# A hybrid decoder step on one core: the sampled sequences' states loaded in both layouts, their update fused, and a second pair of buffers for two evacuation tiles

## The chip, the cores and the metric

The kernel runs on one core of a Trainium2 chip. The metric is the device time of one execution in microseconds (us); lower is better. A matrix product runs on TensorE (PE); VectorE (DVE), ScalarE (ACT) and GpSimd (POOL) work beside it. Loads are issued by SyncE (SP), stores mostly by ACT. Every engine takes its instructions in a fixed order, and a waiting instruction holds up everything behind it on that engine.

## The reference, cut to what matters

One layer is computed for a prompt of 1024 positions and, with the same weights, for 8 sampled sequences of 8 positions each (64 positions). Per layer: a normalised and modulated input, one wide product `h @ w_in`, a pooling branch, a Mamba-2 state-space branch (SSD), and two output products. The change touches only the state-space branch of the samples, where each sequence brings a recurrent state of 32 heads x 64 x 128:

```
acs = cumsum(dt * A)
y   = (C B^T * decay * dt) x   +  (C * exp(acs)) . h        # h: the state before
h   = h * exp(acs_last) + sum_j  B_j  w_in_j  x_j           # the new state, an output
```

`C . h` contracts over the state's 128 columns (n); the update scales the old state by one number per head and sequence and adds an outer product.

## The kernel before, in words

The work is done in stretches one after the other: the input and the first products (to about 120 us), the wide product `h @ w_in` (to about 798 us), the SSD of the prompt in 32 chunks with the output products of the branches woven in (to about 1075 us), and the last products.

The wide product is made in pairs of 128 columns. Each pair is one Strassen step (`strassen`, seven `product`s of 24 matmuls of 272 columns, lines L611 to L613 in before). The results leave PSUM by DVE (and ACT at L654) into four tiles of a pool with one buffer each: `s1`, `u2`, `u3` and `c2`. L622 is `add`, which writes `u2` from `s1` and `u3` from `u2`; L627 is `out`. The four tiles end as the pair's results: ACT applies the gate function to them (L723), and they are stored from there to DRAM (L725). So the next pair may write `u2` only when the store of the pair before has landed. A trace row drops the digits of a name: `u` is `u2` or `u3`, `h` is `h0`, and `whi`/`wlo` are the two halves into which ACT (L168) and POOL (L171) split each weight tile `raw` or `rawA`.

Beside the last ten pairs (`LAST = 10`, about 560 to 798 us) runs the work of the samples. First `dt_end` makes the decays; among others it makes `EbS`, the factor exp(acs_last) of every sequence and head, copied to all partitions (one product of ones, L1141, and one Exp, L1142). Then `ssd_samples` runs for four groups of 8 heads, one step at a time: `samples_beside` is called after each product of a pair and advances it. In a group:

- the decay matrix `dec` is loaded by SP (L1187), masked by two selects on POOL (L1195, L1196), passed through Exp on ACT (L1201), multiplied on DVE (L1249) and used by PE (`inner`, L1213);
- then for each half (4 sequences): the inputs are copied by POOL (L1261), turned by PE (L1264, L1266), and weighted by DVE into `xs` (L1268), `xh` (L1272, L1273) and `Bb` (L1276, L1278). `dec`, `xh` and `Bb` share a ring of three buffers with the tag `dec`;
- the four states of the half lie turned, 128 state columns on the partitions, 512 (head, channel) columns along them. PE multiplies them by `cz` (L1293), DVE scales them by `EbS` (L1298), and then for each sequence PE makes the outer product (L1288), DVE adds it (L1289) and ACT stores the new state (L1290). The states are loaded six tiles ahead (`h0`, `H0B = 6`, L1237), and turned back on the host.

The order on each engine in this stretch is set by a scheduler that simulates a timeline; it follows the code's order, priorities and buffer releases. PE's order and the rest are fixed in the built program.

Of the kernel before, what the change touches and what calls it, by code (L numbers as in the profile page):

```python
# [46 lines left out]
def tile_pool_ssd_step(  # L47
    ctx: ExitStack, tc: tile.TileContext,
    x_prompt, x_sample, state_pool, state_conv, state_ssm, c_prompt, c_sample,
    w_ada, b_ada, norm_g, w_in, conv_w, conv_b, dt_bias, a_log, d_skip, ssm_norm_g,  # L50
# [6 lines left out]
    def nm(s):  # L57
        uid[0] += 1
        return f"{s}_{uid[0]}"
# [38 lines left out]
    def PB():  # L98
        return psB.tile([P, 512], F32, tag="ps", name=nm("ps"))
# [435 lines left out]
    def pair_w(c0, c1, pri, early):  # L535
# [63 lines left out]
        return run  # L599
    prep_q = []  # L600

    turn = [0]
# [463 lines left out]

    H0B = 6


    def dt_end():  # L1070
# [14 lines left out]

        A = sp.tile([P, NH], F32, tag="A", name="A", bufs=1)
# [19 lines left out]
        yield  # L1106
        r, e, q, s2, p = tmp("xd", 2), tmp("xw", 1), tmp("h0", H0B), tmp("h0", H0B), tmp("hT", 1)
        V.tensor_scalar(r, x, 0.0, None, ALU.max)
# [110 lines left out]
    def spt(shape, tag, bufs, dt=F32):  # L1219
        return sp.tile(list(shape), dt, tag=tag, name=nm(tag), bufs=bufs)  # L1220

    def ssd_samples(g):
# [5 lines left out]
        load_E(E2, g)  # L1228
        dec = spt([P, 8, NS], "dec", 3)[:NS]
        decays(dec, g, NC)  # L1230
# [4 lines left out]
        def h0_load(j):  # L1235
            h0 = spt([P, 512], "h0", H0B)
            load(h0, state_ssm[g, j])  # L1237
            h0s[j] = h0
        h0_load(0)
        yield  # L1240
        px = PB()
# [7 lines left out]
        V.tensor_tensor(dec, dec, pc[:S, :S].unsqueeze(1).to_broadcast([S, 8, S]), ALU.mult)  # L1249
        for j in range(1, 4):  # L1250
            h0_load(j)
# [6 lines left out]
        for hf in range(2):  # L1258
# [4 lines left out]
            for q in range(4):  # L1263
# [20 lines left out]

            def update(b):
                h0 = h0s.pop(4 * hf + b)
                pu = PB()
                mm(pu, Bb[:96, b], xh[:96], start=True, stop=True)  # L1288
                V.tensor_tensor(h0, h0, pu, ALU.add)  # L1289
                store_(new_ssm_s[g, 4 * hf + b], h0)  # L1290
            po = PB()
            for b in range(4):
                mm(po[32 * b:32 * b + 32, :], cz[:, b, :], h0s[4 * hf + b], start=True, stop=True)  # L1293
            yo = spt([P, 512], "hT", 1)
            act(yo, po, AF.Copy)
            for b in range(4):
                hv = h0s[4 * hf + b].rearrange("p (h d) -> p h d", d=64)
                V.tensor_tensor(hv, hv, EbS[:, 4 * hf + b, 8 * g:8 * g + 8].unsqueeze(2).to_broadcast([P, 8, 64]), ALU.mult)  # L1298
                if b == 1:
                    yield  # L1300
            yield
            for b in range(4):
                update(b)
                if not hf:
                    h0_load(4 + b)
                if b < 3:
                    yield
# [240 lines left out]
    def to_ssd():  # L1548
        nonlocal right, sd, sp, mask, maskS, blkS, dtT, acT, wdT, wd3, blk3, Elb, EbS
# [10 lines left out]
        EbS = one([P, NB, NH], "EbS")  # L1560
# [6 lines left out]
    sd = sp = mask = maskS = blkS = dtT = acT = wdT = wd3 = blk3 = Elb = EbS = None  # L1567

# [13 lines left out]
    def samples_beside():  # L1582
        due[0] += 1
        if due[0] == 7 * LAST - 4:
            with behind(mybir.EngineType.SP):
                next(p_in)
# [383 lines left out]
    for i in range(8):  # L1970
# [34 lines left out]
        else:  # L2005
# [8 lines left out]

_INS = ['x_prompt', 'x_sample', 'state_pool', 'state_conv', 'state_ssm', 'c_prompt', 'c_sample', 'w_ada', 'b_ada',
        'norm_g', 'w_in', 'conv_w', 'conv_b', 'dt_bias', 'a_log', 'd_skip', 'ssm_norm_g', 'pool_w', 'pool_scale',
        'w_pool_out', 'w_ssm_out', 'w_o', 'final_g']
_OUTS = [((1, 1024, 1024), 'float32'), ((8, 8, 1024), 'float32'), ((512, 15), 'float32'),
         ((24, 128, 3), 'float32'), ((4, 128, 512), 'float32'), ((512, 8, 15), 'float32'),
         ((24, 128, 24), 'float32'), ((4, 8, 128, 512), 'float32')]  # L2020

# [5 lines left out]
def _lay(name, a):  # L2027
    if name == "state_ssm":
        return a.reshape(NB, NG, 512, P).transpose(1, 0, 3, 2)
    if name in ("state_conv", "state_pool"):  # L2030
        return a.reshape(-1, P).T
    return a


def _back(n, a):
    if n == 4:
        return a.transpose(0, 2, 1).reshape(1, 1, NH, 64, P)
    if n == 7:
        return a.transpose(1, 0, 3, 2).reshape(1, NB, NH, 64, P)
    if n == 2:  # L2040
        return a.T.reshape(1, 1, 15, DP)
    if n == 5:
        return a.transpose(1, 2, 0).reshape(1, NB, 15, DP)
    if n in (3, 6):
        return _conv_back(a, n)
    return a

# [19 lines left out]
```

## Time and profile before

| what | us |
|---|---|
| median of 3 runs (lowest to highest) | 1259.33 (1257.79 to 1262.46) |
| the profiled execution, its time | 1258.3 |
| its span in the profile | 1256.6 |
| PE busy | 1223.8 |
| DVE busy | 923.6 |
| ACT busy | 699.4 |
| POOL busy | 681.1 |

Read: PE is nearly always occupied, so the time is set by PE's work and by the places where PE waits or runs at a lower clock. The profiled execution lies 1.0 us under the median of the runs and within their spread.

### The profile page before, as it was taken

The page shows a single profiled execution, that of the slowest core. Times are in us where ns is not written, and L with a number is a line of the kernel's source. Part 1 is how long each engine was busy: PE and PEld are TensorE (multiplying, and loading weights), DVE is VectorE, ACT ScalarE, POOL GpSimd, SP SyncE. Part 2 cuts the span into 40 slices and gives each one's busy share as a digit, 9 for nine tenths or more (in the row PEclk, how much of TensorE's full clock was granted, in tenths as well). Part 3 has the DMA queues.
Part 4 walks back from the last instruction along what each step waited for, and adds up shares of the span by engine and source line. Part 5 has one row for each costly group of instructions (what it writes and reads, how often), then busy time and mean ns, then how long its engine had stood idle before and what let it go on. Part 6 is the DMA issues. An engine that isn't in the chain of part 4 may idle for free. (4 is left out here: it accounts for less than half of the span.)

```text
span 1256.6 us, 25313 instructions
## 1 busy us (share of the span) xinstructions
PE 1223.8 (97%) x9377; PEld 1151.2 (92%) x9377; DVE 923.6 (74%) x1521; ACT 699.4 (56%) x1616; POOL 681.1 (54%) x555
## 2 busy tenths in 40 slices
PE   7999999999999999999899999999999999999998
PEld 6779999999999999998789889999999999999786
DVE  4696689976989588974777776697767879666543
ACT  4675356575666656545444364787887768422211
POOL 1006668877888778664345444465565657455000
PEclk9999999999999999999899999999999999999999
DMA  9836555755555565444456545989666576485431
GB/s 358 264 120 221 138 164 148 199 197 152 159 184 194 162 168 161 152 137 134 147 162 210 168 140 172 330 295 319 207 193 200 181 225 200 144 289 170 151 109 51
DMA packets 208715, 234.85 MB, mean 187 GB/s; under 512 B 41242, under 2 KB 151174, under 8 KB 208591
## 3 DMA queue, kind: packets, MB, share of 16 engines
q1 hardware_dynamic: 154036, 159.51, 41.7%
q10 hardware_dynamic: 54554, 73.72, 17.0%
q8 instruction: 74, 1.21, 0.4%
q14 instruction: 51, 0.41, 0.1%
HBM read 158.56 MB, written 74.62 MB: 186 GB/s over the span
## 5 line engine op out<-in xcount | busy, mean ns | idle before, releaser
L171 POOL TENSOR_TENSOR wlo<-rawA,whi 128x512 fp32r<-128x512 f32 x120 | 190.5, 1593 | 157.4 <-ACT whi L168 79.8
L171 POOL TENSOR_TENSOR wlo<-raw,whi 128x512 fp32r<-128x512 f32 x92 | 150.6, 1644 | 125.2 <-ACT whi L168 115.3
L362 PE MATMUL mm<-Y,whi 128*128 128x352 f32 (+1 forms) x480 | 160.7, 335 | 0.6 <-DVE G L1876 0.2
L363 PE MATMUL mm<-Y,whi 128*128 128x352 f32 (+1 forms) x480 | 158.0, 329 | 0.4 <-DVE Y L1500 0.4
L364 PE MATMUL mm<-Y,wlo 128*128 128x352 f32 (+1 forms) x480 | 157.5, 328 | 0.0
L613 PE MATMUL mm<-Y,wlo 128*128 128x272 f32 x496 | 143.6, 290 | 1.9 <-POOL wlo L171 1.1
L611 PE MATMUL mm<-Y,whi 128*128 128x272 f32 x496 | 144.1, 291 | 0.7 <-ACT whi L168 0.7
L612 PE MATMUL ps<-Y,whi 128*128 128x272 f32 x496 | 143.1, 289 | 0.0
L611 PE MATMUL ps<-Y,whi 128*128 128x272 f32 x496 | 142.9, 288 | 0.0
L613 PE MATMUL ps<-Y,wlo 128*128 128x272 f32 x496 | 142.8, 288 | 0.0
L612 PE MATMUL mm<-Y,whi 128*128 128x272 f32 x496 | 142.4, 287 | 0.0
L1050 DVE SCALAR_TENSOR_TENSOR GA<-GA,cvT,GA 128x1112 f32<-128x1112 f32 x72 | 129.7, 1806 | 0.1
L168 ACT ACTIVATE whi<-rawA 128x512 fp32r<-128x512 f32 x125 | 77.9, 625 | 88.3 <-PE ps L612 44.1
L168 ACT ACTIVATE whi<-raw 128x512 fp32r<-128x512 f32 x96 | 58.9, 627 | 91.5 <-DVE raw L557 47.1
L611 PEld LDWEIGHTS mm<-Y,whi 128*128 128x128 f32 x496 | 93.6, 189 | 3.3 <-ACT whi L168 1.9
L613 PEld LDWEIGHTS mm<-Y,wlo 128*128 128x128 f32 x496 | 93.2, 188 | 2.9 <-POOL wlo L171 1.6
L611 PEld LDWEIGHTS ps<-Y,whi 128*128 128x128 f32 x496 | 93.4, 188 | 1.8 <-DVE c L627 0.8
L362 PEld LDWEIGHTS mm<-Y,whi 128*128 128x128 f32 x480 | 90.6, 189 | 4.1 <-DVE G L1876 2.3
L612 PEld LDWEIGHTS mm<-Y,whi 128*128 128x128 f32 x496 | 93.5, 188 | 0.7 <-issue 0.6
L612 PEld LDWEIGHTS ps<-Y,whi 128*128 128x128 f32 x496 | 93.3, 188 | 0.3
L613 PEld LDWEIGHTS ps<-Y,wlo 128*128 128x128 f32 x496 | 93.2, 188 | 0.0
L363 PEld LDWEIGHTS mm<-Y,whi 128*128 128x128 f32 x480 | 90.8, 189 | 2.7 <-DVE Y L1500 0.9
(440 smaller groups left out, 3760.7 us busy)
## 6 DMA issues: line engine op xcount, KB each, us to landing
rawA<-in_w_in SPq DMA_DIRECT2D x46, 512.0 KB
dec<-acs_d SPq DMA_DIRECT2D x32, 512.0 KB
xbc<-GA ACTq DMA_DIRECT2D x24, 512.0 KB
xb<-xbc SPq DMA_DIRECT2D x32, 384.0 KB
rawA<-in_w_in SPq DMA_DIRECT2D x32, 256.0 KB
pw<-in_w_ssm_out ACTq DMA_DIRECT2D x32, 256.0 KB
ws<-ph ACTq DMA_DIRECT2D x32, 256.0 KB
ws<-pw SPq DMA_DIRECT2D x32, 256.0 KB
```

The lines of the kernel that those rows point to most:

```text
L168: ins = act(hi[:, :, :ncols], raw[:, :, :ncols], AF.Copy)
L171: (eng or nc.gpsimd).tensor_tensor(lo[:, :, :ncols], raw[:, :, :ncols], hi[:, :, :ncols].bitcast(F32), ALU.subtract)
L362: mm(ps[:, :n], a, rh[k][:, o:o + n], start=(k == 0), stop=False)
L363: mm(ps[:, :n], a, rl[k][:, o:o + n], start=False, stop=False)
L364: mm(ps[:, :n], b, rh[k][:, o:o + n], start=False, stop=(k == nk - 1))
L611: mm(p, hi, ah, start=(k == 0), stop=False)
L612: mm(p, hi, al, start=False, stop=False)
L613: mm(p, lo, ah, start=False, stop=(k == 3))
L1050: V.scalar_tensor_tensor(d[:, :n], rp[:, k:k + n], cvT[:, 24 * k + mc:24 * k + mc + 1], d[:, :n], ALU.mult, ALU.add)
```

## The change

The state's tensor is handed to the program twice: `state_ssm` as it is (sequence, head, channel, state column) and `state_turned` in the layout of before. C's products (now L1302) read the turned one, from a new ring of four `hs` tiles, loaded four at a time. The update reads the plain one: a tile is now two heads of four sequences (128 partitions of head and channel, 4 x 128 columns), the outer product has its operands exchanged (L1293), and four SCALAR_TENSOR_TENSOR instructions (L1296) do `h0 * factor + product` in one pass, one for each sequence, with the factor taken as one number per partition from `E2`, a tile that is loaded anyway. The scaling by `EbS` and `EbS` itself go. The new state is written in the plain layout.

Room is made: `h0` has 5 buffers instead of 6, the `dec` ring 2 instead of 3, `yo` moves into the tag `xw`, `A` into `cz`, and the tile `p` of `dt_end` into `yt`. Of every two pairs beside the samples one takes `u2` and `u3` from a second place (`vu2`, `vu3`), except the last pair.

```diff
     def strassen(w, d0, d1, early=False):
         def tmp(tag):
+            if tag in ("u2", "u3") and beside[0] % 2 and beside[0] < LAST - 1:
+                return sp.tile([P, 2, SB], F32, tag="v" + tag, name=nm(tag), bufs=1)
             return pa.tile([P, 2, SB], F32, tag=tag, name=nm(tag))
...
-    H0B = 6
+    H0B = 5
...
-        own = tmp("xd", 2)[:NS, :256]
-        V.tensor_tensor(own.rearrange("p (b h) -> p b h", h=NH), a[:NS, 256:F].unsqueeze(1).to_broadcast([NS, NB, NH]),
-                        blk.unsqueeze(2).to_broadcast([NS, NB, NH]), ALU.mult)
-        pe = PB()
-        mm(pe[:, :256], ones[:NS], own, start=True, stop=True)
-        act(EbS.rearrange("p b h -> p (b h)"), pe[:, :256], AF.Exp, scale=-1.0)
...
-        dec = spt([P, 8, NS], "dec", 3)[:NS]
+        dec = spt([P, 8, NS], "dec", 2)[:NS]
...
         def h0_load(j):
-            h0 = spt([P, 512], "h0", H0B)
-            load(h0, state_ssm[g, j])
+            hf, q = divmod(j, 4)
+            h0 = spt([P, 4, P], "h0", H0B)
+            load(h0, state_ssm[0, 4 * hf:4 * hf + 4, 8 * g + 2 * q:8 * g + 2 * q + 2].rearrange("b h p n -> (h p) b n"))
             h0s[j] = h0
+        hts = {}
+
+        def turned_load(hf):
+            for b in range(4):
+                hts[b] = spt([P, 512], "hs", 4)
+                load(hts[b], state_turned[g, 4 * hf + b])
         h0_load(0)
+        turned_load(0)
...
-            xh = spt([P, 512], "dec", 3, F32R)
+            xh = spt([P, 512], "dec", 2, F32R)
...
-            Bb = spt([P, 4, P], "dec", 3, F32R)
+            Bb = spt([P, 4, P], "dec", 2, F32R)
...
-            def update(b):
-                h0 = h0s.pop(4 * hf + b)
+            def update(r):
+                h0 = h0s.pop(4 * hf + r)
                 pu = PB()
-                mm(pu, Bb[:96, b], xh[:96], start=True, stop=True)
-                V.tensor_tensor(h0, h0, pu, ALU.add)
-                store_(new_ssm_s[g, 4 * hf + b], h0)
+                mm(pu, xh[:96, r * P:(r + 1) * P], Bb[:96].rearrange("p b n -> p (b n)"), start=True, stop=True)
+                for b in range(4):
+                    cc_ = 32 * hf + 8 * b + 7
+                    V.scalar_tensor_tensor(h0[:, b, :], h0[:, b, :], E2[:, r, cc_:cc_ + 1],
+                                           pu[:, b * P:(b + 1) * P], ALU.mult, ALU.add)
+                store_(new_ssm_s[0, 4 * hf:4 * hf + 4, 8 * g + 2 * r:8 * g + 2 * r + 2]
+                       .rearrange("b h p n -> (h p) b n"), h0)
             po = PB()
             for b in range(4):
-                mm(po[32 * b:32 * b + 32, :], cz[:, b, :], h0s[4 * hf + b], start=True, stop=True)
-            yo = spt([P, 512], "hT", 1)
+                mm(po[32 * b:32 * b + 32, :], cz[:, b, :], hts[b], start=True, stop=True)
+            if not hf:
+                turned_load(1)
+            yo = spt([P, 512], "xw", 1)
             act(yo, po, AF.Copy)
-            for b in range(4):
-                hv = h0s[4 * hf + b].rearrange("p (h d) -> p h d", d=64)
-                V.tensor_tensor(hv, hv, EbS[:, 4 * hf + b, 8 * g:8 * g + 8].unsqueeze(2).to_broadcast([P, 8, 64]), ALU.mult)
-                if b == 1:
-                    yield
             yield
```

The scheduler sets the whole stretch anew. Outside about 540 to 800 us the order on all engines is as before. Three places matter for the prediction. First DVE in the second half of group 0, before. `xw` is `xs`, `dec` at L1273 and L1278 are `xh` and `Bb`, `u2`, `s1` and `c2` are tiles of a pair:

```order
L1268 TENSOR_TENSOR xw_1276_8230<-ps_1274_8223,wd3_7194 96x512
L1276 TENSOR_TENSOR bt_1278_8235<-ps_1275_8228,bt_1278_8235 32x128
L1273 TENSOR_TENSOR dec_1277_8232<-xw_1276_8230,dec_1277_8232 32x512
L1278 TENSOR_TENSOR dec_1279_8238<-bt_1278_8235,blk3_7195 96x512
L1298 TENSOR_TENSOR h0_1252_8113<-h0_1252_8113,EbS_7197 128x512
L1298 TENSOR_TENSOR h0_1254_8119<-h0_1254_8119,EbS_7197 128x512
L1298 TENSOR_TENSOR h0_1266_8174<-h0_1266_8174,EbS_7197 128x512
L1298 TENSOR_TENSOR h0_1270_8211<-h0_1270_8211,EbS_7197 128x512
L622 TENSOR_TENSOR u2_1286_8252<-s1_1285_8251,ps_1294_8306 128x272
L1289 TENSOR_TENSOR h0_1252_8113<-h0_1252_8113,ps_1295_8322 128x512
```

and the same place on DVE now (L1273, L1278, L1281 and L1283 are before's L1268, L1273, L1276 and L1278, and L625 is L622):

```order
L1273 TENSOR_TENSOR xw_1281_8246<-ps_1279_8239,wd3_7194 96x512
L1281 TENSOR_TENSOR bt_1283_8251<-ps_1280_8244,bt_1283_8251 32x128
L1283 TENSOR_TENSOR dec_1284_8254<-bt_1283_8251,blk3_7195 96x512
L1278 TENSOR_TENSOR dec_1282_8248<-xw_1281_8246,dec_1282_8248 32x512
L1296 SCALAR_TENSOR_TENSOR h0_1259_8129<-h0_1259_8129,hst_1214_7886,ps_1298_8306 128x128 x4
L625 TENSOR_TENSOR u2_1293_8275<-s1_1292_8274,ps_1301_8329 128x272
L1296 SCALAR_TENSOR_TENSOR h0_1261_8138<-h0_1261_8138,hst_1214_7886,ps_1302_8343 128x128 x4
L1296 SCALAR_TENSOR_TENSOR h0_1273_8196<-h0_1273_8196,hst_1214_7886,ps_1303_8350 128x128 x4
```

The four passes with `EbS` are gone from between `Bb` and the next pair's `u2`, and the updates follow at once.

Second, SP's queue at the start of group 1, with the waits of each load, before (`dec_8505` is group 1's decay matrix, `h` a state, `hst` the group's inputs):

```order
L1237 DMA h_1270_8211<-in_state_ssm 128x512 [waits DMAHW4_49,DMAHW0_49,DVE_49]
L1237 DMA h_1326_8521<-in_state_ssm 128x512 [waits DMAHW3_49,DVE_49]
L543 DMA rawA_8577<-in_w_in 128x4x256 [waits Pool_49]
L1237 DMA h_1330_8533<-in_state_ssm 128x512 [waits DMAHW5_49,DMAHW1_49,DVE_49]
L1225 DMA hst_8500<-xbc_175 128x6x64 [waits DMAHW2_49,PE_49,Pool_49]
L1187 DMA dec_8505<-acs_d 64x8x64 [waits PE_49]
L1237 DMA h_1331_8535<-in_state_ssm 128x512 [waits DMAHW6_49,DMAHW4_49,DVE_49]
```

and now, with the four turned loads ahead of it:

```order
L1235 DMA h_1332_8547<-in_state_ssm 128x4x128 [waits DMAHW4_49,DVE_49]
L1222 DMA hst_8526<-xbc_175 128x6x64 [waits Pool_49]
L1242 DMA hs_8549<-in_state_turned 128x512 [waits DMAHW2_49,PE_49]
L1242 DMA hs_8551<-in_state_turned 128x512 [waits DMAHW3_49,PE_49]
L1242 DMA hs_8553<-in_state_turned 128x512 [waits PE_49]
L1242 DMA hs_8555<-in_state_turned 128x512 [waits DMAHW5_49,PE_49]
L1184 DMA dec_8531<-acs_d 64x8x64 [waits DMAHW0_49,PE_49]
L1235 DMA h_1340_8567<-in_state_ssm 128x4x128 [waits DMAHW6_49,DMAHW2_49,DVE_49]
```

Both wait for PE, but not for the same matmul: with three buffers `dec` took the place of the first half's `Bb`; with two it takes that of the second half's `xh`, which PE reads until the last update of the group before.

Third, POOL at the group-0 decay, before:

```order
L171 TENSOR_TENSOR wlo_7784<-raw_7677,whi_7783 128x512
L1195 AFFINE_SELECT dec_7895<-dec_7895 64x512
L171 TENSOR_TENSOR wlo_7788<-rawA_7545,whi_7787 128x512
L1196 AFFINE_SELECT dec_7895<-dec_7895 64x512
L171 TENSOR_TENSOR wlo_7855<-rawA_7850,whi_7854 128x512
```

and now:

```order
L171 TENSOR_TENSOR wlo_7778<-raw_7676,whi_7777 128x512
L1192 AFFINE_SELECT dec_7889<-dec_7889 64x512
L1193 AFFINE_SELECT dec_7889<-dec_7889 64x512
L171 TENSOR_TENSOR wlo_7782<-rawA_7544,whi_7781 128x512
L171 TENSOR_TENSOR wlo_7849<-rawA_7844,whi_7848 128x512
```

The two selects now stand together, and one weight split has moved behind them.

More of the change, by code (lines that the diff above doesn't have):

```diff
@@ L600, in tile_pool_ssd_step @@
     prep_q = []
+    beside = [0]
     turn = [0]
@@ L1249, in ssd_samples @@
         V.tensor_tensor(dec, dec, pc[:S, :S].unsqueeze(1).to_broadcast([S, 8, S]), ALU.mult)
-        for j in range(1, 4):
+        for j in range(1, 3):
             h0_load(j)
@@ L1283, in ssd_samples @@
             yield
[L1285 to L1286 removed]
+            def update(r):
+                h0 = h0s.pop(4 * hf + r)
                 pu = PB()
[L1288 to L1290 removed]
+                mm(pu, xh[:96, r * P:(r + 1) * P], Bb[:96].rearrange("p b n -> p (b n)"), start=True, stop=True)
[5 more added lines that the diff above has]
+                       .rearrange("b h p n -> (h p) b n"), h0)
             po = PB()
             for b in range(4):
[L1293 to L1294 removed]
+                mm(po[32 * b:32 * b + 32, :], cz[:, b, :], hts[b], start=True, stop=True)
+            if not hf:
+                turned_load(1)
+            yo = spt([P, 512], "xw", 1)
             act(yo, po, AF.Copy)
[L1296 to L1306 removed]
+            yield
+            for q in range(4):
+                j = 4 * hf + q
+                update(q)
+                if j + 3 < 8:
+                    h0_load(j + 3)
+                if q < 3:
                     yield
@@ L1548, in to_ssd @@
     def to_ssd():
-        nonlocal right, sd, sp, mask, maskS, blkS, dtT, acT, wdT, wd3, blk3, Elb, EbS
+        nonlocal right, sd, sp, mask, maskS, blkS, dtT, acT, wdT, wd3, blk3, Elb
         right.__exit__(None, None, None)
@@ L1559, in to_ssd @@
         wd3, blk3, Elb = one([96, 2, NH], "wd3"), one([96, 4], "blk3"), one([P, NC, NH], "Elb")
-        EbS = one([P, NB, NH], "EbS")
         right = tc.tile_pool(name="sp", bufs=2, side="right", reuse_waits="tile")
@@ L1566, in tile_pool_ssd_step @@
     right_all = []
-    sd = sp = mask = maskS = blkS = dtT = acT = wdT = wd3 = blk3 = Elb = EbS = None
+    sd = sp = mask = maskS = blkS = dtT = acT = wdT = wd3 = blk3 = Elb = None
     first()
@@ L1583, in samples_beside @@
         due[0] += 1
+        beside[0] = int(due[0]) // 7
         if due[0] == 7 * LAST - 4:
@@ L2045, in _back @@
         return _conv_back(a, n)
+    if n == 4:
+        return a.transpose(0, 2, 1).reshape(1, 1, NH, 64, P)
     return a
@@ L2056 @@
     for name in _INS:
-        a = _np.ascontiguousarray(_lay(name, _np.asarray(inputs[name])))
+        a = _np.ascontiguousarray(_lay(name, _np.asarray(inputs["state_ssm" if name == "state_turned" else name])))
         arrays[f"in_{name}"] = a
```

18 lines of the change are left out of this document (7 added, 11 removed).

## The prediction, made before the changed kernel ran

> **What bounds the kernel now.** I read the page first, then the busy times by stretches of 40 us, then PE's waits in the stretch that the change touches. The page says that PE is occupied:
>
> ```profile
> PE 1223.8 (97%) x9377; PEld 1151.2 (92%) x9377; DVE 923.6 (74%) x1521; ACT 699.4 (56%) x1616; POOL 681.1 (54%) x555
> ```
>
> The columns below are the stretch and its length, busy time (and instructions) of PE, weight loads, DVE, ACT and POOL, granted clock, share of the DMA engines, GB/s.
>
> ```profile
> 520.00:560.00 40.00, 40.00 (x322) 39.99 (x321) 32.09 (x54) 21.04 (x44) 28.05 (x28) 1.00 0.48 157
> 560.00:600.00 40.00, 36.61 (x285) 33.97 (x283) 21.83 (x48) 22.11 (x46) 16.00 (x13) 0.98 0.44 131
> 600.00:640.00 40.00, 35.64 (x244) 30.98 (x240) 33.36 (x55) 17.57 (x38) 16.62 (x13) 0.90 0.45 141
> 720.00:760.00 40.00, 36.32 (x289) 33.90 (x288) 29.53 (x55) 22.72 (x48) 19.24 (x16) 1.00 0.43 148
> 840.00:880.00 40.00, 40.00 (x332) 37.81 (x331) 30.90 (x51) 29.32 (x78) 22.49 (x26) 1.00 0.94 314
> ```
>
> Before and after the samples' stretch PE is full; in it PE is idle some 10% of several rows, and at 600 to 640 the clock is below 1.00. Nothing there is full: DVE has 22 to 33 of 40 us. So PE waits for latency, for chains of small instructions in a fixed order, and what can be won is what it waits. PE's waits from 560 to 800 us, and the three stretches with a lower clock:
>
> ```profile
> PE ps L1213 <- DVE dec L1249: 3.1, 2, 2.3
> PE ps L1288 <- DVE u L622: 2.8, 1, 2.8
> PE ps L1288 <- DVE dec L1273: 2.7, 2, 1.3
> PE mm L613 <- POOL wlo L171: 1.8, 4, 0.7
> PE ps L1245 <- ACT s L654: 1.4, 1, 1.4
> PE mm L611 <- ACT whi L168: 0.8, 1, 0.8
> PE ps L1288 <- DVE h L1289: 0.2, 1, 0.2
> ...
> 590.00:600.00 10.00, 6.61 (x58) 5.95 (x56) 4.10 (x10) 8.85 (x21) 4.68 (x4) 0.90 0.65 184
> 600.00:610.00 10.00, 9.58 (x60) 7.10 (x57) 7.72 (x15) 3.37 (x8) 1.49 (x1) 0.76 0.08 29
> 630.00:640.00 10.00, 7.74 (x48) 7.43 (x48) 9.61 (x20) 6.32 (x15) 3.56 (x4) 0.83 0.52 156
> ```
>
> The waits add up to 12.8 us. The clock costs at most 10 x (0.10 + 0.24 + 0.17) = 5.1 us more. Some 18 us are thus all that this change can win; PE's own work hardly changes.
>
> The clock fell after the two longest waits, the first and second row here, and not after the others:
>
> ```profile
> 599.13 0.59 PE L1213 MATMUL ps<-dec,xd 64*64 64x64 f32 x6 [2.35 <-DVE dec L1249]
> 632.26 0.79 PE L1288 MATMUL ps<-dec,dec 96*128 96x512 f32 x1 [2.81 <-DVE u L622]
> 741.08 0.68 PE L1213 MATMUL ps<-dec,xd 64*64 64x64 f32 x16 [0.74 <-DVE dec L1249]
> ```
>
> The Trainium skill (TensorE: Matmul & The Clock Gate, "What's actually happening") has the clock halved after an idle window of about 3.4 us. By that rule waits of 2.35 and 2.81 us would leave it alone, and the 3.4 us of clock in my sum would stay lost; the trace shows it falling after them, so the measurement decides.
>
> **Why DVE is late there.** These are DVE's groups of 560 to 800 us (count, busy us, mean ns, idle before), then single instructions:
>
> ```profile
> L1298 DVE TENSOR_TENSOR h<-h,EbS 128x512 f32<-128x512 f32 x32 | 29.6, 982 | 0.4 <-PE ps L1293 0.3
> L1289 DVE TENSOR_TENSOR h<-h,ps 128x512 f32<-128x512 f32 x32 | 21.1, 676 | 1.9 <-PE ps L1288 1.9
> L622 DVE TENSOR_TENSOR u<-s,mm 128x272 f32<-128x272 f32 x9 | 3.9, 436 | 21.7 <-DMA gp<-u 10.3 <-DMA z<-u 5.4 <-DMA gs<-u 5.3
> ...
> 619.93 0.44 DVE L622 TENSOR_TENSOR u<-s,mm 128x272 f32<-128x272 f32 x1 [3.74 <-DMA z<-u]
> 623.85 6.73 DVE L1298 TENSOR_TENSOR h<-h,EbS 128x512 f32<-128x512 f32 x4
> 738.36 0.44 DVE L622 TENSOR_TENSOR u<-s,mm 128x272 f32<-128x272 f32 x1 [8.23 <-DMA gp<-u]
> ```
>
> Two things: DVE stands 21 us for `u2`, whose last store has not landed, and the scaling passes take 29.6 us. Before 632.26 both come together: 3.74 us for `u2`, then 6.73 for four passes.
>
> **The change part by part.** The rows that price DVE's work (ns least, median, most):
>
> ```profile
> L1298 DVE TENSOR_TENSOR h<-h,EbS x32: 676/682/3811, 603.4 to 767.9; 128x512 f32<-128x512 f32 x32
> L1289 DVE TENSOR_TENSOR h<-h,ps x32: 623/675/690, 609.7 to 776.4; 128x512 f32<-128x512 f32 x32
> L1312 DVE TENSOR_TENSOR yt<-ps,hst x8: 275/279/285, 615.1 to 777.0; 128x128 f32<-128x128 f32 x8
> L1316 DVE TENSOR_TENSOR xd<-xd,yt x8: 277/294/810, 615.4 to 777.6; 128x128 f32<-128x128 f32 x8
> ```
>
> Out go 29.6 + 21.1 = 50.7 us. In come 128 SCALAR_TENSOR_TENSOR of 128x128 with one operand in PSUM. The trace has none with a PSUM operand; the nearest row is L1312, same size, one operand in PSUM: 128 x 0.279 = 35.7 us. As the other end I take L1298's stretching, mean over least: 128 x 0.277 x 982 / 676 = 51.5. I take 35.7: rows with a PSUM operand (L1289, L1312) spread by 11% at most, those with both in SBUF stretch up to 5.6-fold (L1298) and 2.9-fold (L1316). So DVE gains 15 us, the longest pieces above all, or nothing.
>
> The Trainium skill (SBUF — State Buffer, "Who interferes with whom") says that a DVE instruction with two SBUF inputs contends with a GpSimd instruction that reads SBUF; the trace agrees, 3811 ns at most in L1298 against 690 in L1289. It does not say whether a per-partition factor in SBUF counts as the second input; if it did, the upper end would hold and DVE would gain nothing.
>
> *The wait for group 0's decay, 2.35 us, and the clock behind it.* By the order 93 product matmuls stand between L1245 and L1213 now, 76 before: 17 x 40 / 322 = 2.1 us of cover. The lost `EbS` steps shorten the chain too. Gain 2.35. But on POOL both selects now come ahead of a weight split that PE waited for already:
>
> ```profile
> 589.74 0.62 SPq L1187 DMA_DIRECT2D dec<-acs_d  x1
> 592.87 1.09 POOL L1195 TENSOR_SCALAR_AFFINE_SELECT dec<-dec 64x512 f32<-64x512 f32 x1 [0.17 <-DMA dec<-acs_d]
> 595.16 1.10 POOL L1196 TENSOR_SCALAR_AFFINE_SELECT dec<-dec 64x512 f32<-64x512 f32 x1
> ```
>
> That split is 1.1 us later: loss 1.1. Of the clock (3.4 here) I take half, 1.7. Net +2.95.
>
> *632.26.* Both causes go (a second `u2`, no passes): 2.81 + 1.7 of clock = +4.5.
>
> *The two waits for `xh` (2.7).* L1273 no longer stands behind the passes: +2.7. But the first update now follows C's products after 12 product matmuls (1.5 us) in both halves of group 0, where 36 and 14 stood; I take 0.5 us lost in each. Net +1.7.
>
> *736 to 741 us.* The 0.74 stood behind the 8.23 us for `u2`; the 1.4 is a PSUM bank that waits for ACT, which now has one table change fewer there: +2.1.
>
> *The weight waits, 1.8 + 0.8:* half of what is left beside the one above, +0.8. *The `EbS` product on PE:* one product less, which runs as two matmuls of 256 columns; at 40 / 322 = 0.124 us for one of 272 columns that is +0.25.
>
> *The ring of two.* Group 1 to 3's decay load now waits for PE's last update of the group before. From there: load 592.87 - 0.17 - 589.74 = 3.0; two selects 2.2 and one instruction between them 1.2; table 1.28 and Exps 2.0 (below); product 0.7, as L1289; sum 10.4 us. PE has 106 to 113 product matmuls in between by the order, 13.2 us or more. So PE needn't wait; ACT and POOL may, in order, with weight splits behind them. I take 0.8 us for each group, -2.5.
>
> ```profile
> 679.06 1.28 ACT L1201 ACT_TABLE_LOAD   x1 [0.45 <-ACT u L723]
> 680.36 0.35 ACT L1201 ACTIVATE dec<-dec,acT 64x64 f32<-64x64 f32 x1
> 682.05 0.34 ACT L1201 ACTIVATE dec<-dec,acT 64x64 f32<-64x64 f32 x1
> ```
>
> *Transfers.* 32 turned loads of 256 KB are 8.4 MB more; at 600 to 640 us a share of 0.45 moved 141 GB/s, so they add 27 us of all engines over 200, 0.13 to a share of some 0.5. The states now move in pieces of 512 bytes, which costs the issuing engine 0.2 us more each (L1386, such pieces, against L1290):
>
> ```profile
> L1386 SPq DMA_DIRECT2D sz<-z x32: 518/530/1559, 799.5 to 1071.2; - x32
> L1290 ACTq DMA_DIRECT2D out<-h x32: 338/344/891, 610.4 to 777.1; - x32
> ...
> SPq L543 <- POOL wlo L171: 188.2, 34, 17.7
> SPq L1237 <- DMA out<-h: 107.7, 22, 18.5
> ```
>
> On ACT that is 6.4 us of 240 in which it works about half: hidden by its idle time. On SP the 32 turned loads stand ahead of weight loads, which already wait for free buffers (first row), so they are early; the state loads wait for stores to land (second row), now with five buffers. If that cover went, DVE's updates would wait, and PE behind them. I count 0.
>
> Sum: 2.95 + 4.5 + 1.7 + 2.1 + 0.8 + 0.25 - 2.5 = 9.8 us. From the profiled execution, 1258.3, that gives 1248.5; the median of the runs lies 1.0 higher, so for a median I say 1249.5. About 0.5%, 6.3 us, is what a measurement of this kernel can tell from no change.
>
> **The rivals.**
>
> *DVE is not relieved* (51.5 us of updates). For: the factor is read from SBUF, and POOL works in the stretch. Against: L1289's narrow spread. Left are the start, half of 632, 0.74 and the -2.5: 2.95 + 2.25 + 0.74 - 2.5 = 3.4, so 1256. Chance 0.15.
>
> *The new order brings its own waits:* all eight halves wait about 1.3 us for `xh`, as 2.7 / 2 shows, because the updates stand so close behind. For: 12 product matmuls are 1.5 us and the chain has five instructions on three engines. Against: the last six halves have 12 to 31 between and DVE is emptier. 9.8 + 1.0 - 8 x 1.3 = 0.4, so 1259. Chance 0.13.
>
> *The ring of two makes it slower.* If the chain of 10.4 us takes 16, PE waits 2.8 at three group starts and loses 1.7 of clock each, 13.5 in all, and the gain of 12.3 without this term is gone; from there on it is slower, and at 18 by 3 x 6.5 - 12.3 = 7.2 us, 1266.5. For: POOL and ACT take it in order, behind weight splits and gate functions, and the turned loads are in the queue just ahead. Against: 3 us of slack and 0.13 more of DMA. Chance 0.12, of which 0.08 is slower by over 0.5%.
>
> **How the numbers follow.** My forecast has the remaining 0.60, with a range of its own from 1242 to 1253. Everything won would be 1259.3 - 12.8 - 5.1 - 0.25 = 1241, the low end; the high end takes in the first two rivals and leaves out the third: 1259. Faster by over 0.5% (under 1253): 0.60 and a third of the first rival, 0.65; slower: 0.08 and 0.02 of the second rival, 0.10; the rest, 0.25, within.
>
> **What would show it.** Right: no L1298; the new updates at about 280 ns with little spread; the idle time before the first `u2` of a pair gone except in the last pair; no wait of 2 us or more at L1213 or at the update matmul, and clock 1.00 from 600 to 640; the samples' stretch some 10 us shorter, the others as long as before. Wrong: waits of PE at L1213 of groups 1 to 3 behind the decay's load; update matmuls that wait for `xh`; updates stretched while POOL works; or POOL and ACT standing at the decay with weight splits late behind them.

## The result, and the profile after

The changed kernel takes 1245.1 us in the median (1241.7 to 1249.0, 4 runs) against 1259.9 for the kernel before on the same chip: a ratio of 0.9883, 95% interval 0.9846 to 0.9919. Two later comparisons gave 0.9906 [0.9888, 0.9924] and 0.9914 [0.9894, 0.9933]. So it is faster by about 1%, 11 to 15 us; the forecast was 1249.5. The profiled execution took 1249.0 us, the longest of the first four.

PE stays the bound, with 2.9 us less of occupied time:

```profile
PE 1220.9 (98%) x9375; PEld 1148.8 (92%) x9375; DVE 912.6 (73%) x1584; ACT 694.1 (56%) x1611; POOL 678.2 (54%) x555
```

The same stretches as before (columns: stretch and length, busy time of PE, weight loads, DVE, ACT, POOL, granted clock, DMA share, GB/s):

```profile
560.00:600.00 40.00, 38.09 (x296) 34.72 (x294) 22.58 (x52) 20.23 (x45) 17.06 (x14) 0.96 0.45 125
600.00:640.00 40.00, 39.62 (x315) 35.63 (x308) 30.82 (x78) 22.85 (x50) 22.22 (x18) 1.00 0.84 256
640.00:680.00 40.00, 39.32 (x306) 37.45 (x305) 29.66 (x72) 12.70 (x26) 16.12 (x15) 1.00 0.80 246
680.00:720.00 40.00, 37.83 (x277) 34.03 (x277) 26.86 (x66) 19.30 (x44) 15.30 (x13) 0.91 0.64 195
720.00:760.00 40.00, 40.00 (x325) 37.24 (x324) 27.41 (x69) 20.67 (x46) 21.57 (x18) 1.00 0.60 181
...
590.00:600.00 10.00, 8.09 (x65) 6.23 (x63) 3.93 (x9) 6.14 (x17) 4.66 (x4) 0.84 0.60 157
600.00:610.00 10.00, 10.00 (x79) 9.15 (x72) 9.07 (x23) 3.92 (x8) 3.61 (x3) 0.98 0.65 208
```

From 600 to 640 PE has 39.62 us of work at full clock, where it had 35.64 at 0.90; 720 to 760 is full. Two stretches have a lower clock than before: 560 to 600, with 0.96 (0.98 before), and 680 to 720, with 0.91 (1.00 before). PE's waits from 560 to 800 us:

```profile
PE ps L1210 <- DVE dec L1254: 2.1, 1, 2.1
PE mm L614 <- POOL wlo L171: 1.8, 2, 1.7
PE ps L1293 <- DVE dec L1278: 0.9, 2, 0.7
PE mm L363 <- DVE Y L1507: 0.4, 1, 0.4
```

They add up to 5.2 us, against 12.8. (L1210 is the inner product, L1293 the update matmul, L614 a product with the low part of a weight; L1213, L1288 and L613 before.) DVE's new updates, and the first `u2` of a pair (ns least, median, most; then one update's four; then busy us, mean ns, idle before):

```profile
L1296 DVE SCALAR_TENSOR_TENSOR h<-h,hst,ps x128: 334/342/349, 604.8 to 766.0; 128x128 f32<-128x128 f32 x128
...
604.82 1.11 DVE L1296 SCALAR_TENSOR_TENSOR h<-h,hst,ps 128x128 f32<-128x128 f32 x4
...
L1296 DVE SCALAR_TENSOR_TENSOR h<-h,hst,ps 128x128 f32<-128x128 f32 x128 | 35.1, 340 | 5.2 <-PE ps L1293 5.2
L625 DVE TENSOR_TENSOR u<-s,mm 128x272 f32<-128x272 f32 x9 | 3.9, 431 | 5.9 <-ACT whi L168 5.7
```

The updates have hardly any spread, and no store stands before `u2` any more.

The wait of 2.1 us is that of group 2's decay. Its chain, from the load's issue to PE (start, us, engine, line, operation, idle time before):

```profile
669.17 1.97 SPq L1184 DMA_DIRECT2D dec<-acs_d  x1
...
675.71 1.09 POOL L1192 TENSOR_SCALAR_AFFINE_SELECT dec<-dec 64x512 f32<-64x512 f32 x1 [4.72 <-DMA dec<-acs_d]
...
679.25 1.09 POOL L1193 TENSOR_SCALAR_AFFINE_SELECT dec<-dec 64x512 f32<-64x512 f32 x1
...
682.93 2.02 ACT L1198 ACTIVATE dec<-dec,acT 64x64 f32<-64x64 f32 x8
...
685.77 1.12 PE L1210 MATMUL ps<-dec,xd 64*64 64x64 f32 x16 [2.12 <-DVE dec L1254]
```

The load is issued at 669.17 and the first select can start at 675.71; two weight splits stand between the selects. From issue to PE it is 16.6 us. Behind this wait the clock falls, to 0.78 from 680 to 690 and 0.88 from 690 to 700: 10 x (0.22 + 0.12) = 3.4 us. In the second and third profile of the changed kernel the wait is 1.4 and 1.2 us, and the clock stays at 1.00 from 680 to 720.

All kernels of the study, with all their runs (those of the kernel before are of the three later comparisons). The last two columns split the mean time: what the mean granted clock leaves out of 1250 us, and the rest.

| kernel | runs | median us | ratio to before, 95% | clock lost, us | rest, us |
|---|---|---|---|---|---|
| before | 51 | 1257.7 | 1 | 8.4 | 1249.1 |
| after | 14 | 1245.5 | 0.9883, 0.9906, 0.9914 | 3.7 | 1242.0 |
| before, second `u2`, `u3` only | 12 | 1258.9 | 1.0004 [0.9991, 1.0017] | 6.9 | 1251.7 |
| before, no passes | 6 | 1248.2 | 0.9932 [0.9916, 0.9948] | 5.6 | 1243.1 |
| before, ring of two | 11 | 1255.2 | 0.9980 [0.9972, 0.9989] | 7.2 | 1247.6 |
| layout, ring of three | 11 | 1255.2 | 0.9976 [0.9961, 0.9992] | 6.3 | 1248.2 |
| layout, ring of three, decay held | 6 | 1251.4 | 0.9949 [0.9929, 0.9969] | 6.9 | 1243.5 |
| layout, ring of two | 12 | 1248.9 | 0.9930 [0.9908, 0.9952], 0.9939 [0.9919, 0.9958] | 4.7 | 1244.4 |
| after, ring of three, four states | 6 | 1250.7 | 0.9942 [0.9930, 0.9955] | 5.0 | 1245.5 |
| after, inner product later | 6 | 1247.0 | 0.9922 [0.9904, 0.9941] | 3.8 | 1244.2 |
| after, one split on DVE | 6 | 1247.1 | 0.9920 [0.9903, 0.9938] | 4.4 | 1242.4 |

Of the 11.7 us between the means of before and after (1257.4 and 1245.7) some 7 are waits and work and 4.7 are clock. That the clock came back because the waits went is shown only in part. By stretches of 20 us, the profile of the kernel before loses 5.2 us of clock from 560 to 800, and the three of the changed kernel lose 5.2, 1.8 and 0. The profile before loses another 1.7 us at 1090 to 1110 (0.99 and 0.84), where the order is the same in both kernels and no wait of PE is listed; the three of the changed kernel lose nothing there.

### The profile page after: what moved, and what is told of

Read it like the earlier page. It is cut to its first block, busy times and chain, and to the rows that moved or that the text cites. A ratio compares the mean times of both kernels' runs of the same rounds, so it can differ in the third digit from the quotient of the medians.

```text
span 1247.3 us, 25450 instructions
## 1 busy us (share of the span) xinstructions
PE 1220.9 (98%) x9375; PEld 1148.8 (92%) x9375; DVE 912.6 (73%) x1584; ACT 694.1 (56%) x1611; POOL 678.2 (54%) x555
## 5 line engine op out<-in xcount | busy, mean ns | idle before, releaser
L614 PE MATMUL mm<-Y,wlo 128*128 128x272 f32 x496 | 143.7, 290 | 2.8 <-POOL wlo L171 2.0
L613 PE MATMUL ps<-Y,whi 128*128 128x272 f32 x496 | 143.7, 290 | 0.0
L614 PE MATMUL ps<-Y,wlo 128*128 128x272 f32 x496 | 143.3, 289 | 0.0
L613 PE MATMUL mm<-Y,whi 128*128 128x272 f32 x496 | 142.5, 287 | 0.0
L614 PEld LDWEIGHTS mm<-Y,wlo 128*128 128x128 f32 x496 | 93.3, 188 | 4.6 <-POOL wlo L171 2.5
L613 PEld LDWEIGHTS mm<-Y,whi 128*128 128x128 f32 x496 | 93.5, 188 | 0.8 <-issue 0.6
L613 PEld LDWEIGHTS ps<-Y,whi 128*128 128x128 f32 x496 | 93.8, 189 | 0.2
L614 PEld LDWEIGHTS ps<-Y,wlo 128*128 128x128 f32 x496 | 93.8, 189 | 0.0
```

The source lines that it names most:

```text
L613: mm(p, hi, al, start=False, stop=False)
L614: mm(p, lo, ah, start=False, stop=(k == 3))
```

## Experiments

**The second buffers alone.** The kernel before, with this in `strassen` (and the counter `beside` of the pairs):

```diff
+            if tag in ("u2", "u3") and beside[0] % 2 and beside[0] < LAST - 1:
+                return sp.tile([P, 2, SB], F32, tag="v" + tag, name=nm(tag), bufs=1)
             return pa.tile([P, 2, SB], F32, tag=tag, name=nm(tag))
```

> The kernel before, with the second buffers for u2 and u3 alone; layout, scaling passes and ring of three stay. Account of the prediction (each of the two causes would do at 632, the passes alone make the other waits): DVE no longer stands 3.7 us at 619.9, so the wait of 2.8 us at the update of 632 and half or all of its clock (1.7 to 3.4 us) go, and of the waits at 736 and 741 some 2 us: 5 to 8 us faster, ratio 0.994 to 0.996; the wait for group 0's decay (2.35) and the two for xh (1.3 each at 677 and 723) stay. Rival 1, the stores of u2 are the whole cause: the 21.7 us of DVE's idle time go and with them nearly all of the 14.8 us, ratio 0.988. Rival 2, the scaling passes are the whole cause: the passes take the freed time, 1 us at most, ratio 0.999 to 1.0.

1.0004: nothing, as the second rival had it. DVE's timeline and PE's wait there show why:

```profile
615.31 0.44 DVE L626 TENSOR_TENSOR u<-s,mm 128x272 f32<-128x272 f32 x1 [0.27 <-PE mm L615]
...
619.03 0.44 DVE L631 TENSOR_TENSOR c<-u,mm 128x272 f32<-128x272 f32 x1 [1.86 <-PE mm L615]
...
622.19 6.61 DVE L1302 TENSOR_TENSOR h<-h,EbS 128x512 f32<-128x512 f32 x4
...
629.99 0.44 DVE L626 TENSOR_TENSOR u<-s,ps 128x272 f32<-128x272 f32 x1
...
PE ps L1292 <- DVE u L626: 2.4, 1, 2.4
```

`u2` comes 4.6 us earlier than before (615.31, not 619.93), but the passes start only 1.7 us earlier (622.19, not 623.85), for what stands ahead of them waits for PE (1.86 us in the second row). They still take 6.6 us, and PE still waits 2.4 us for the `u2` behind them.

**The passes alone.** The kernel before with these lines taken out, so that the old states are not multiplied by their decay:

```diff
             act(yo, po, AF.Copy)
-            for b in range(4):
-                hv = h0s[4 * hf + b].rearrange("p (h d) -> p h d", d=64)
-                V.tensor_tensor(hv, hv, EbS[:, 4 * hf + b, 8 * g:8 * g + 8].unsqueeze(2).to_broadcast([P, 8, 64]), ALU.mult)
-                if b == 1:
-                    yield
+            yield
             yield
```

> The kernel before without the 32 scaling passes of L1298 (the old state is not multiplied by its decay; the product for EbS, all loads, stores, updates and the single buffers of u2 and u3 stay). The run with second buffers alone gave 1.0004, so the account in which u2's stores share the cause at 632 has fallen. Theory 'passes': all four halves of groups 0 to 3 lose DVE's longest pieces (29.6 us): the wait at 632 (2.8 and 1.7 to 3.4 of clock) and the two for xh (2.7) go, the wait for group 0's decay (2.35) stays: 7 to 9 us faster than before, ratio 0.993 to 0.9945, about what layout without second buffers gave (0.993). Rival 'not the passes but the new order and shorter start': 2 us at most, ratio above 0.998.

0.9932, where the theory said 0.993 to 0.9945. Of PE's waits the one at 632 is gone and that of group 0's decay stays (2.3; the other, group 3's, is 1.2 at 732 where it was 0.74 at 741); but those for `xh` (L1273) hardly shrink, 2.2 for 2.7:

```profile
PE ps L1213 <- DVE dec L1249: 3.6, 2, 2.3
PE ps L1288 <- DVE dec L1273: 2.2, 2, 1.1
```

So the passes made 632, and without them most of what the change wins is won, but they did not make the waits for `xh`. Ahead of one of the two waits, in group 1, the subtraction that ends `xh` is slow itself; ahead of the other it takes its 0.68 us, in both kernels. The rows of the kernel before (all eight subtractions, then the slow one, then POOL beside it) stand first, and the slow one without passes second.

```profile
L1273 DVE TENSOR_TENSOR dec<-xw,dec x8: 682/683/3565, 606.0 to 764.4; 32x512 fp32r<-32x512 f32 x8
...
674.12 3.56 DVE L1273 TENSOR_TENSOR dec<-xw,dec 32x512 fp32r<-32x512 f32 x1
...
671.63 3.27 POOL L1195 TENSOR_SCALAR_AFFINE_SELECT dec<-dec 64x512 f32<-64x512 f32 x1 [2.66 <-DMA dec<-acs_d]
674.88 1.28 POOL L171 TENSOR_TENSOR wlo<-rawA,whi 128x512 fp32r<-128x512 f32 x1
676.12 1.09 POOL L1196 TENSOR_SCALAR_AFFINE_SELECT dec<-dec 64x512 f32<-64x512 f32 x1
```

```profile
664.27 2.57 DVE L1273 TENSOR_TENSOR dec<-xw,dec 32x512 fp32r<-32x512 f32 x1
```

Its median is 0.68 us; in the second no passes stand anywhere, and it is slow all the same. POOL was in a select when the slow one began, and went on without a gap. That holds throughout: the 14 profiles of this study have 112 of these subtractions; the 15 that took 1.39 to 3.57 us all began while POOL was in a select, a weight split or a difference of its own, and none of the 97 that took 0.68 or 0.69 us did.

**Layout and fused update without second buffers** (the kernel after without the rule above), run twice:

> The kernel after without the second buffers of u2 and u3; layout, fused update and ring of two stay. Account of the prediction: start 2.95 + 632 4.5 + xh 1.7 + weights 0.8 + EbS product 0.25 - ring 2.5 = 7.7 us faster than before, ratio 0.994, and DVE again stands some 20 us before u2. Rival 1 (stores of u2 are the whole cause): no faster than before, ratio 0.999 to 1.002. Rival 2 (passes are the whole cause): as fast as after, ratio 0.988.

> Layout, fused update and ring of two without second buffers, once more, beside the changed kernel: 0.992 to 0.994 if the second buffers are worth 2 to 3 us, within 0.002 of the changed kernel's ratio if they are worth nothing.

> The changed kernel a third time, beside layout only on one chip. So far 0.988 and 0.991 against 0.993 for layout only. If second buffers of u2 and u3 are worth some 2 to 3 us once the passes are gone: 0.987 to 0.991 here, and 0.992 to 0.994 for layout only. If they are worth nothing: both within 0.002 of each other.

0.9930 and 0.9939, as the forecast's account had it; in the one comparison where both ran beside each other, layout only gave 0.9939 and the changed kernel 0.9914, just above the window of 0.987 to 0.991. Over all runs the means lie 3.4 us apart (1249.1 and 1245.7, with a standard error of about 1 us of the difference). The intervals touch in each single comparison; the traces show where it comes from. Layout only, around the first `u2` of group 0's second half:

```profile
614.61 0.44 DVE L623 TENSOR_TENSOR u<-s,mm 128x272 f32<-128x272 f32 x1 [4.00 <-DMA z<-u]
...
615.68 0.63 ACT L1275 ACTIVATE dec<-xw 96x512 fp32r<-96x512 f32 x1 [2.79 <-DVE xw L1271]
616.33 1.28 ACT L724 ACT_TABLE_LOAD   x1
...
617.96 0.61 ACT L168 ACTIVATE whi<-rawA 128x512 fp32r<-128x512 f32 x1
...
618.62 0.39 PE L612 MATMUL mm<-G,whi 128*128 128x272 f32 x1 [3.34 <-ACT whi L168]
```

DVE stands 4.0 us for a store of `u2`; behind it `xs` is late, so ACT's copy of it is late, and with it the weight split that ACT has behind a gate function and a table change; PE waits 3.3 us for that split. In the changed kernel's three profiles this wait is 0 to 0.2 us. With the passes in the way the second buffers won nothing; without them they win about 3 us.

**The ring of three in the changed kernel** (four state buffers in place of five make the room):

```diff
-    H0B = 5
+    H0B = 4
...
-        dec = spt([P, 8, NS], "dec", 2)[:NS]
+        dec = spt([P, 8, NS], "dec", 3)[:NS]
```

and the same for `xh` and `Bb`.

> The kernel after with three buffers in the ring of dec, xh and Bb, as before the change; to make room the states get four buffers in place of five. Theory 'the ring of two gives back a part': the decay of groups 1 to 3 is loaded half a group earlier, the wait of 2.1 us at the inner product of group 2 (685.8) goes and the 6.8 us at half clock (3.4 us) behind it: 2 to 5.5 us faster than after, ratio to before 0.984 to 0.987. Rival 'the clock falls anyway': the wait goes but another one takes its place, time as after, 0.988. Rival 'four state buffers are too few': state loads wait for the stores, updates late on DVE, PE waits at products behind them, 2 us or more slower than after.

0.9942: slower than the changed kernel by some 4 us, though the wait at 685 is gone. That was the opposite of the theory, so three more kernels went after it. **The ring of two alone, in the kernel before:**

> The kernel before with the ring of dec, xh and Bb cut from three buffers to two, nothing else. Theory 'the ring of two costs a wait and a stretch of low clock': the decay's load of groups 1 to 3 waits for the last update of the group before, PE waits some 2 us at one to three inner products and may lose 3.4 us of clock behind each: 2 to 13 us slower, ratio 1.002 to 1.010. Rival 'the chain of 10 to 18 us is covered or the wait only moves': same time, ratio 0.999 to 1.001.

0.9980 [0.9972, 0.9989]: faster, against both, by 2.5 us in the mean. In its profile the waits of 1.4 and 0.74 us at 736 and 741 are gone, 0.9 of the 2.7 for `xh` is left and 0.8 of the 2.8 at 632; new are 1.9 for `u2` at 758 and 0.6 at 646. The waits for weights fall only from 2.6 to 1.7. **Layout only, with the ring of three and five state buffers:**

> The changed kernel without second buffers of u2 and u3 (as layout only, 0.993), and in their room the ring of three for dec, xh and Bb; five state buffers, so that the run with four (0.9942) is told apart from the ring. Theory 'the ring of two gives back a part': 2 to 5 us faster than layout only, 0.989 to 0.991. Theory 'four state buffers were what cost, the ring nothing': 0.992 to 0.994. Rival 'an earlier decay load pushes selects and exponentials ahead of weight splits': slower, 0.994 to 0.996.

0.9976 against 0.9930 and 0.9939 with two: the ring of three costs 5 to 6 us, not the state buffers. ACT's timeline with the ring of three (the kernel with four state buffers), around group 3's decay, and PE there:

```profile
716.46 1.07 ACT L1198 ACTIVATE dec<-dec,acT 64x64 f32<-64x64 f32 x4
717.55 1.28 ACT L726 ACT_TABLE_LOAD   x1
718.84 0.43 ACT L726 ACTIVATE s<-s 128x272 f32<-128x272 f32 x1
719.29 1.28 ACT L1198 ACT_TABLE_LOAD   x1
...
721.55 1.13 ACT L168 ACTIVATE whi<-raw 128x512 fp32r<-128x512 f32 x2
...
722.22 0.39 PE L612 MATMUL mm<-Y,whi 128*128 128x272 f32 x1 [1.47 <-ACT whi L168]
723.57 0.39 PE L614 MATMUL mm<-Y,wlo 128*128 128x272 f32 x1 [0.83 <-POOL wlo L171]
```

The same weight split and the same exponentials in the changed kernel (its second profile):

```profile
716.32 1.15 ACT L168 ACTIVATE whi<-raw 128x512 fp32r<-128x512 f32 x2 [0.50 <-DVE raw L557]
...
728.94 1.31 ACT L1198 ACTIVATE dec<-dec,acT 64x64 f32<-64x64 f32 x5
```

With three buffers the decay is there early, so its exponentials stand ahead of the split, in two pieces with a gate function between them, and the split comes some 5 us later. The table changes from 560 to 800 us (count, busy us, mean ns), ring of three first and the changed kernel second:

```profile
L726 ACT ACT_TABLE_LOAD x10 | 12.8, 1283 | 0.6 <-ACT u L726 0.4
L1198 ACT ACT_TABLE_LOAD x8 | 10.3, 1283 | 1.3 <-DVE u L625 0.8 <-ACT u L726 0.4
```

```profile
L726 ACT ACT_TABLE_LOAD x6 | 7.7, 1283 | 0.5 <-ACT u L726 0.4
L1198 ACT ACT_TABLE_LOAD x4 | 5.1, 1283 | 0.6 <-DMA dec<-acs_d 0.6
```

Eight more of 1.28 us, 10.3 us of ACT. With five state buffers (layout only, ring of three) it is four more than with the ring of two, and the same pair of waits for a weight, 1.48 and 0.83 us, stands at 729 and 730. In the kernel before, whose ring of three cost 2.5 us, it is only one more (13 and 12).

**The ring of three with the decay held back.** Layout only, three buffers, but the next group's `dec` is first written by DVE out of the last updated state:

```diff
+                elif j == 7 and g < 3:
+                    nxt[g + 1] = spt([P, 8, NS], "dec", 3)[:NS]
+                    V.tensor_copy(nxt[g + 1][:1, 0, :1], last[0][:1, 0, :1])
```

> Layout with the ring of three (0.9976), but the decay's load of groups 1 to 3 is held back: its buffer is first written by a one-partition copy on DVE out of the last updated state of the group before, so it can't be loaded sooner than with the ring of two. In the order the exponentials of each group then stand in one piece behind the weight splits, as with the ring of two; with the free ring of three they stand ahead of them, in two groups in pieces with further table loads. Theory 'with three buffers the decay comes early, and its selects and exponentials stand ahead of weight splits that PE waits for': the loss goes, ratio 0.991 to 0.994, no pair of waits for weights near 730. Rival 'the third buffer itself costs (xh or Bb earlier, other places)': 0.996 to 0.998.

0.9949 [0.9929, 0.9969]: between the two windows, with an interval that reaches into both. The table changes are back at 6 and 4, the pair of waits near 730 is gone, and the time without the clock's share is that of the ring of two (1243.5, against 1244.4, and 1248.2 with the ring free). The clock's share is not back (6.9 us, against 4.7; six runs). So the early decay is shown for the pair of waits, 2.3 us of the 5 to 6; that nothing else in the ring of three costs time is not.

**The inner product one step later,** in the changed kernel:

```diff
             act(t[:, q], xb[:, q], AF.Copy, scale=Dv[:, 4 * g + q:4 * g + q + 1])
         yield
+        yield
```

> The kernel after with one more step between the scaling of t by D and the inner product, so that all of a group's later work stands one step (some 3 us of products) later; ring of two. Theory 'the chain behind the ring of two is about 2 us too long for its cover': 3 us more cover take away the wait of 2.1 us at 685.8 and the clock behind it, as the ring of three does: 2 to 5.5 us faster than after, ratio to before 0.984 to 0.987. Rival 'cover is given back': the chain starts at the last update of the group before, which moves by one step as well but only once per group, so from group 1 on load and inner product move by the same amount plus one step; if instead POOL's place in order sets it, the wait stays and the time is as after, 0.988.

0.9922: no faster. The wait at 685 goes, and others come in (1.4 us for group 1's decay at 639, 2.1 for `xh` at 667). The extra step changed the order of the whole group, so it doesn't test the cover alone.

**One weight split moved to DVE,** in the changed kernel; and the changed kernel once more beside other comparisons:

```diff
                 add(t2)
-                add(b22)
+                add(b22, n == 22)
```

where the flag lets `split` take DVE for the low part.

> The changed kernel with one weight split (the one whose low part PE waits for at 595, behind the two selects of group 0's decay) moved from POOL to DVE, which stands idle there for 4.3 us. Theory 'group 0 is bound by its decay chain': the wait of 1.65 us at the product goes, PE comes to the inner product 1.65 us earlier and waits there for DVE's decay product instead, which ends at the same time: time as the changed kernel (0.988 to 0.991). Rival 'the split is the bound': 1.7 us faster and with it 1.7 us of clock, 0.986 to 0.988.

> The changed kernel once more, so that it stands beside the others on one chip with more runs. First comparison 0.9883 [0.9846, 0.9919] from 4 runs; layout without second buffers gave 0.993 [0.991, 0.995]. If the second buffers are worth something once the passes are gone: 0.987 to 0.990. If they are worth nothing, as with the kernel before: 0.992 to 0.994, and the first four runs were on the low side.

0.9920 for the moved split, the changed kernel's time within the interval. The changed kernel itself gave 0.9906, between the two windows named for it. The wait moved as the first theory said. With the split on POOL (the changed kernel's second profile):

```profile
594.69 0.40 PE L614 MATMUL mm<-Y,wlo 128*128 128x272 f32 x1 [1.65 <-POOL wlo L171]
596.28 1.00 PE L1210 MATMUL ps<-dec,xd 64*64 64x64 f32 x16
...
595.55 0.68 DVE L1254 TENSOR_TENSOR dec<-dec,ps 64x512 f32<-64x512 f32 x1 [4.29 <-ACT dec L1198]
```

and on DVE:

```profile
596.65 1.12 PE L1211 MATMUL ps<-dec,xd 64*64 64x64 f32 x16 [2.39 <-DVE dec L1255]
...
590.30 1.37 DVE L171 TENSOR_TENSOR wlo<-rawA,whi 128x512 fp32r<-128x512 f32 x1 [1.83 <-ACT whi L168]
...
595.92 0.68 DVE L1255 TENSOR_TENSOR dec<-dec,ps 64x512 f32<-64x512 f32 x1 [3.21 <-issue]
```

DVE's decay product ends at 596.2 and at 596.6, and in both PE starts the inner product just then. Group 0's start is bound by its decay chain; the wait for the weight lies inside it. No version here beats the changed kernel.

## Why the prediction was right, point by point

Sign and range held; the time is 4 us below the forecast. By its terms, in the first profile after:

- *Group 0's decay, +2.95.* Right in sum. From 590 to the inner product PE waits 1.8 us, for weight splits (second row of its waits), where it was 1.0 for splits and 2.35 for the decay: 1.6 won. The clock lost from 590 to 610 is 10 x (0.16 + 0.02) = 1.8 us, not 3.4: 1.6 won, together 3.2. The two steps inside it were not right: the decay chain still sets the start, as the moved split shows, so the wait for the decay did not go but lies behind the wait for the late split, and the split costs nothing of its own. And the clock's part is chance: the third profile loses none there.
- *632.26, +4.5.* The size was right: at the update (618.2) PE now waits 0.2 us, and from 600 to 640 the clock is 1.00. The step "both causes go" was half wrong: the second `u2` alone leaves 2.4 us of it; without the passes nothing of it is left.
- *`xh`, +1.7.* In sum right, 0.9 us is left of 2.7. The reason, that L1273 stands behind the passes, failed: without passes 2.2 us stay, and with them, but with the ring of two, 0.9. In layout only it was 1.8 and 3.7 us, in the changed kernel 0.9, 1.6 and 1.6. The subtraction is slow in just those halves in which POOL is at work when it begins; no run moved POOL's work to test that.
- *736 to 741, +2.1.* Right in size: PE has no wait from 720 to 760. The reasons given are not singled out: in the kernel before the ring of two alone takes both waits away, and the second buffers alone 1.7 us of them.
- *Weights +0.8, `EbS` product +0.25.* All that is left for weights, 1.8 us, lies at the start; the 1.6 elsewhere are gone, so the term was half of what came. PE has two matmuls fewer (9375, 9377); what they save was not measured.
- *The updates at 0.279 us.* One takes 0.342 us, 23% more, but four that follow one another overlap: four end after 1.11 us, and 128 fill 35.1 us, against 35.7 taken. They do not stretch, so the first rival is out. The Trainium skill (SBUF — State Buffer, "Who interferes with whom") left open whether a per-partition factor in SBUF counts as a second SBUF input; with 334 to 349 ns while POOL is at work 22 of 40 us it does not show here.
- *The ring of two, -2.5.* The term that failed, by its sign. The chain was sized at 10.4 us and measures 16.6 from the issue: the load took 6.5 us, not 3.0, and two splits stand between the selects. The 3.0 came from group 0's load, during which the DMA share was 0.32; in the same profile the loads of groups 2 and 3 took 4.9 and 3.5 us at 0.75 and 0.64, and the load of 6.5 us had a share of about 1.0. So PE did wait at group 2, 2.1 us and 3.4 of clock in the first profile, as the third rival had it, though at one group start and not at three. But the ring of three costs more: 5 to 6 us in the new layout, of which 2.3 are shown to be the early decay's selects and exponentials ahead of weight splits, and 2.5 in the kernel before, mostly by other waits. The working priced the wait that the ring adds, and not what the earlier load pushes back. Put at zero, this term gives 1247.0 in place of 1249.5; at the +2.5 measured in the kernel before, 1244.5, though a part of that lies in waits that other terms count.
- *Transfers, 0.* Right for PE: no update waits for a state's load. The share at 600 to 640 rose from 0.45 to 0.84, more than the 0.13 added on average, while from 680 to 720 it hardly did (0.62 to 0.64): the loads come in bursts. That the late decay is their price fits the times above, but no run took the turned loads away.
- *The second buffers.* Counted only within 632 and 736; they are worth about 3 us, though only once the passes are gone.

The clock was in the sum with 3.4 of the 5.1 us that stood behind the waits, and 4.7 us came back in the mean of all runs. That these are near each other is in part luck: in the first profile the stretch loses as much clock as before (5.2 us), only elsewhere, and a part of the 4.7 lies outside the stretch.

## What to carry to other kernels

A buffer that is free earlier is not always a gain: with engines that take their work in order, an early load puts its whole chain (here selects, table changes and exponentials) ahead of work that the bounding engine needs sooner (2.3 us of waits are shown here), so price what the early chain pushes back as well as the wait it saves. Where two causes stand before one wait, take each away alone: here one sufficed and the other was worth nothing until the first was gone. And when a wait lies inside a longer chain, moving it elsewhere only renames it, as the moved split showed.

## What the runs showed of the hardware that was not expected

The clock falls after some waits and not after others of the same length. The wait of 1.65 to 1.66 us at 595 is in all three profiles of the changed kernel; from 590 to 600 the clock was 0.84 and 0.83 in the first two. The second and the third:

```profile
590.00:600.00 10.00, 8.07 (x60) 5.55 (x58) 3.96 (x9) 5.94 (x16) 4.57 (x4) 0.83 0.55 147
```

```profile
590.00:600.00 10.00, 8.21 (x72) 6.45 (x71) 4.19 (x10) 6.88 (x19) 4.67 (x4) 1.00 0.60 158
```

In layout only a wait of 3.3 us at 618.6 left the clock at 1.00, and one of 2.4 at 711 took it to 0.83 for 10 us. The rule that the prediction cited from the Trainium skill (TensorE: Matmul & The Clock Gate), an idle window of about 3.4 us, would have left the clock alone after all of these waits. It also fell where no wait of PE is listed at all, at 1100 to 1110 in the kernel before (0.84). So the runs of one kernel spread: those of the changed kernel have mean clocks of 0.993 to 0.999 and times of 1250.2 to 1241.7 us, the longer times with the lower clocks. In these traces a wait of some 2 us costs its length and a chance of 1.7 to 3.4 us of clock.

Another is the subtraction above: 0.68 us when POOL stood as it began, and 1.39 to 3.57 us when POOL was at work. The third is that DVE instructions with an operand in PSUM and a factor per partition take 0.34 us each but follow one another 0.26 us apart: four end after 1.11 us, and (1.11 - 0.34) / 3 = 0.26.
